# Two norms of a decoder step: the mean over channels as one product of a sum of seven chunks and one product of the eighth chunk

## The chip, the core and the metric

The kernel runs on one core of one Trainium2 chip. The metric is the device time of one execution in microseconds, the median of three runs. The profiled execution is a further one, recorded instruction by instruction; its times are microseconds from its own start.

## The reference

One step of a two-layer decoder trunk over 512 new prompt tokens and 8 x 4 sample tokens, width 1024. The part that matters here is the first layer's convolution module and the norm behind it:

```python
def rms_norm(x, g):
    return x * lax.rsqrt(jnp.mean(x * x, axis=-1, keepdims=True) + EPS) * g

def layer_norm(x, g, b):
    mu = jnp.mean(x, axis=-1, keepdims=True)
    var = jnp.mean(jnp.square(x - mu), axis=-1, keepdims=True)
    return (x - mu) * lax.rsqrt(var + EPS) * g + b

def conformer_conv(h, past, w_in, b_in, w_dw, b_dw, ln_g, ln_b, w_out, b_out):
    a, gate = jnp.split(h @ w_in + b_in, 2, axis=-1)
    ext = jnp.concatenate([past, a * jax.nn.sigmoid(gate)], axis=1)
    y = causal_dwconv(ext, w_dw, b_dw)                  # width 31, each channel by itself
    y = jax.nn.silu(layer_norm(y, ln_g, ln_b))
    return y @ w_out + b_out, ext[:, -(CONV_WIDTH - 1):]
...
x = x + conformer_conv(rms_norm(x, norm_mix[0]), ...)
x = x + conv_ffn(rms_norm(x, norm_ffn[0]), ...)
# layer 1: stick-breaking attention over paged keys and values, and again conv_ffn
```

## The kernel before

Activations lie transposed: 1024 channels are 8 chunks of 128 partitions, and the 544 tokens are the free dimension, cut into two streams, SA of 256 tokens (h = 0) and SB of 288 tokens (h = 1). A product in full precision is three passes of matmuls on the split operands whi, wlo (weights) and XH, XL (activations); lines L730 to L732 issue them, 8 chunks x 3 for one output chunk of one stream. Weights arrive by DMA as `raw`, ScalarE casts the high part (L374) and VectorE subtracts it for the low part (L377).

The first stage, some 200 us, is written down as a list of operations with dependencies and estimated costs (`plan.op(engine, cost, ...)`), and `Plan.run` puts them in order: at each step it takes the operation that can start earliest by the estimates, weighted by urgency and by the length of the chain behind it. Each engine then executes its own list strictly in that order. So an operation added or removed anywhere can move others, on all engines. What follows the stage (two ConvFFNs, the attention, the last norm) is ordered by plans of its own.

In the stage, for each chunk c and stream h:

- four products at a time (`conv_in`) give two chunks of `a` and two of the gate; L763, L765, L767 and L769 multiply, apply the sigmoid and write the result into `ext_p` (L773 for the sample tokens, `glu_s`).
- The depthwise convolution of chunks 0 and 1 is done on VectorE by 31 taps (L814, L818). Chunks 2 to 7 go through TensorE: `shifted` writes the chunk to DRAM (L832) and reads it back four times shifted into `rep` (L836), and `conv_tensor` multiplies 32 blocks by small diagonal weights `wdg` (L867, 32 matmuls of 32 columns, in two halves of 16); ScalarE copies the result out of PSUM (L872). Sample tokens are convolved on VectorE (L791, L796, with a bias on ScalarE, L798).
- The result `y` replaces `ext_p`. `add_sum` adds the chunks into `ysum` on VectorE (L884, seven adds per stream), and `layer_norm` takes the mean over channels by one product of `ysum` with a matrix of 1/1024 (L900), subtracts it (L908), squares on ScalarE (L910), adds pairs of squares (L915) and multiplies them with the same matrix (L918, four products). Then come the square root (L922), the reciprocal (L924), eight multiplies (L929), Silu (L931) and the split into XH and XL (L933, L934), which the output product `conv_out` reads (L730 to L732 again, evacuated by L1224 into xT).
- The norm in front of the ConvFFN squares xT (L1205 in `normed`), adds the squares up, on GpSimd and the last of a stream on VectorE (L1212), and for stream SA multiplies the sum with the matrix of 1/1024 (L1235). The second stream's norm is finished in the ConvFFN's plan.

PSUM tiles have tags: `acc` (four banks) for products, `tr` (two) for means and variances, `av` (two) for convolutions.

Of the kernel before, what the change touches and what calls it, by code (L numbers as in the profile page):

```python
# [19 lines left out]
NC = D // P  # L20
# [44 lines left out]
LIFT = 10  # L65
# [161 lines left out]
def tile_trunk(  # L227
# [9 lines left out]
    dve, act, pool, pe = nc.vector, nc.scalar, nc.gpsimd, nc.tensor  # L237

    def open_pool(name, bufs=1, space=None, side=None):
        kw = dict(name=name, bufs=bufs, reuse_waits="tile")  # L240
        if space is not None:
            kw["space"] = space
        if side is not None:
            kw["side"] = side
        cm = tc.tile_pool(**kw)
        return cm, cm.__enter__()
# [151 lines left out]
    mean_m = base.tile([P, P], F32, name="mean_m")  # L398
# [26 lines left out]
    def pcol(row, c):  # L425
        return prm[:, c, row:row + 1]
# [174 lines left out]
    yc = ext_p  # L601
# [8 lines left out]
    start_cm, start = open_pool("start")  # L610
# [84 lines left out]
    plan = Plan(E_CONV, 0.12)  # L695
    STREAMS = (SA, SB)
    late = {}

    def buf(pool_, tag, shape, bufs):
        name = pool_ if isinstance(pool_, str) else None  # L700
        b = plan.tile(tag, bufs, lambda: late.get(name, pool_).tile(shape, F32, tag=tag, name=uid(tag), bufs=bufs))
        if name:
            b.after |= {late["op"]}
        return b
# [3 lines left out]
    def psum(tag):  # L708
        def make():
            if tag == "acc":  # L710
                taken.append(tag)
            return bank(tag, uid(tag))

        return plan.tile(tag, banks[tag], make)

    def on(eng, n, dve_cost, pool_cost):
        return (dve, "dve", 0.08 + n * dve_cost) if eng == "dve" else (pool, "pool", 0.1 + n * pool_cost)
# [157 lines left out]

    def add_sum(c, h):
        c0, n = STREAMS[h]
        if c == 0:
            return
        keys = [("y", i, k) for i in ((0, 1) if c == 1 else (c,)) for k in ((1, 2) if h else (0,))]  # L880

        def add():
            o = late["ysum"][:, c0:c0 + n]
            dve.tensor_tensor(o, yc[:, c, c0:c0 + n], yc[:, 0, c0:c0 + n] if c == 1 else o, op=ALU.add)  # L884

        plan.op("dve", 0.08 + n * 1.05e-3, add, r=keys, w=[("sum", h)])

    def table(name):
        plan.op("act", 1.3, lambda: act_table(name), w=["table"])

    def layer_norm(h):

        c0, n = STREAMS[h]
        cols = slice(c0, c0 + n)
        urgent = URGENT
        mu, va = psum("tr"), psum("tr")
        rs = buf("ctmp", "dwa", [P, SEQ], 2)
        ycut = [("y", c, k) for c in range(NC) for k in ((1, 2) if h else (0,))]
        per = len(ycut) // NC
        plan.op("pe", n * 1.68e-3, lambda: pe.matmul(  # L900
            mu()[:, :n], mean_m, late["ysum"][:, cols], start=True, stop=True),
                r=[("sum", h)], w=[mu], urgent=urgent, lift=0.0 if h else LIFT)
        for c in range(NC):
            y = yc[:, c, cols]
            keys = ycut[c * per:(c + 1) * per]
            first = c % SQUARES == 0
            sq = buf("ctmp", "sqn", [P, SB[1]], 3)
            plan.op("dve", 0.1 + n * 1.12e-3, lambda y=y: dve.tensor_tensor(y, y, mu()[:, :n], op=ALU.subtract),  # L908
                    r=[mu], w=keys, urgent=urgent)
            plan.op("act", 0.1 + n * 0.9e-3, lambda y=y, sq=sq: act.activation(sq()[:, :n], y, AF.Square),  # L910
                    r=keys, w=[sq], urgent=urgent)
            if first:
                acc = sq
            else:
                plan.op("dve", 0.08 + n * 1.05e-3, lambda sq=sq, acc=acc: dve.tensor_tensor(  # L915
                    acc()[:, :n], sq()[:, :n], acc()[:, :n], op=ALU.add), r=[sq], w=[acc], urgent=urgent)
            if (c + 1) % SQUARES == 0:
                plan.op("pe", n * 1.68e-3, lambda c=c, acc=acc: pe.matmul(  # L918
                    va()[:, :n], mean_m, acc()[:, :n], start=(c < SQUARES), stop=(c == NC - 1)),
                    r=[acc], w=[va], urgent=urgent)  # L920
        table("sqrt_and_others")
        plan.op("act", 0.1 + n * 0.95e-3, lambda: act.activation(  # L922
            rs()[:, :n], va()[:, :n], AF.Sqrt, bias=eps_t[:, 0:1], scale=1.0), r=[va, "table"], w=[rs], urgent=urgent)
        plan.op("dve", 0.1 + n * 6.2e-3, lambda: dve.reciprocal(rs()[:, :n], rs()[:, :n]), w=[rs], urgent=urgent)  # L924
        table("silu_and_others")
        for c in range(NC):
            y = yc[:, c, cols]
            keys = ycut[c * per:(c + 1) * per]
            plan.op("dve", 0.08 + n * 1.05e-3, lambda y=y: dve.tensor_tensor(y, y, rs()[:, :n], op=ALU.mult),  # L929
                    r=[rs], w=keys, urgent=urgent)  # L930
            plan.op("act", 0.25 + n * 0.9e-3, lambda c=c, y=y: act.activation(  # L931
                y, y, AF.Silu, bias=pcol(R_LNB, c), scale=pcol(R_LNG, c)), r=["table"], w=keys)
            plan.op("act", 0.1 + n * 0.82e-3, lambda c=c, y=y: act.copy(XH[:, c, cols], y), r=keys, w=[("XH", c, h)])  # L933
            plan.op("dve", 0.08 + n * 1.05e-3, lambda c=c, y=y: dve.tensor_tensor(  # L934
                XL[:, c, cols], y, XH[:, c, cols], op=ALU.subtract), r=[("XH", c, h), *keys], w=[("XL", c, h)])
# [142 lines left out]
    for c in range(0, NC, 2):  # L1078
# [9 lines left out]
        for cc in range(2):  # L1088
            plan.op("act", 0.33, lambda c=c, cc=cc, pt=pt: act.copy(
                ext_s[:, c + cc, :, 0:PAST], pt()[:, cc * 240:(cc + 1) * 240].rearrange("p (b t) -> p b t", b=NB)),  # L1090
                r=[pt, "junk"], w=[("past", c + cc)])
# [40 lines left out]
    for h in range(2):  # L1132
        for c in range(NC):
            add_sum(c, h)

    layer_norm(0)

    def state(new):
# [22 lines left out]
    nrm = Norm(R_FFN, later=True)  # L1161
# [39 lines left out]
    def normed(c, h):  # L1201

        c0, n = STREAMS[h]
        sq = plan.tile("sq" if c else "sqa", 2, lambda: nrm.tile("sq" if c else "sqa", 2))
        plan.op("act", 0.1 + n * 0.9e-3, lambda: act.activation(sq()[:, :n], xT[:, c, c0:c0 + n], AF.Square),  # L1205
                r=[("x", c, h), "norm"], w=[sq])
        if c == 0:
            nrm.acc[h] = sq
            return
        a = nrm.acc[h]  # L1210
        e, name, cost = on("dve" if c == NC - 1 else "pool", n, 1.05e-3, 2.25e-3)
        plan.op(name, cost, lambda: e.tensor_tensor(a()[:, :n], sq()[:, :n], a()[:, :n], op=ALU.add), r=[sq], w=[a])  # L1212
# [3 lines left out]
    for h, (c0, n) in enumerate(STREAMS):  # L1216
        if h:
            layer_norm(1)
        for g in (0, 4):
            for i in range(4):  # L1220
                c = g + i
                pt = product(s0 + c, h)
                x = xT[:, c, c0:c0 + n]
                plan.op("dve", 0.1 + n * 1.12e-3, lambda c=c, n=n, x=x, pt=pt: dve.scalar_tensor_tensor(  # L1224
                    x, pt()[:, :n], pcol(R_BOUT, c), x, op0=ALU.add, op1=ALU.add), r=[pt, ("x0", c, h)], w=[("x", c, h)])
                normed(c, h)
        if not h:
            state(False)
            state(True)
            for f0 in (0, 8, 16):  # L1230
                ffn_rows(f0, min(8, NF - f0))
    table("sqrt_and_others")
    ms, rs = psum("tr"), plan.tile("rstd", 2, lambda: nrm.tile("rstd", 2))
    n = SA[1]
    plan.op("pe", 0.53, lambda: pe.matmul(ms()[:, :n], mean_m, nrm.acc[0]()[:, :n], start=True, stop=True),  # L1235
            r=[nrm.acc[0]], w=[ms])
    plan.op("act", 0.34, lambda: act.activation(rs()[:, :n], ms()[:, :n], AF.Sqrt, bias=eps_t[:, 0:1], scale=1.0),
            r=[ms, "table"], w=[rs])
    plan.op("dve", 1.7, lambda: dve.reciprocal(rs()[:, :n], rs()[:, :n]), w=[rs])
    for c in range(NC):  # L1240
# [3 lines left out]
                r=[rs, ("x", c, 0)], w=[u])  # L1244
# [4 lines left out]
            r=[u, ("XH", c, 0)], w=[("XL", c, 0)], lift=NLIFT)  # L1249
# [802 lines left out]
    plan = Plan()  # L2052
# [433 lines left out]
    for i, tag in enumerate(("acc", "z", "z", "one")):  # L2486
# [3 lines left out]
        for q in range(4):  # L2490
            last = plan.op("pe", 6 * SA[1] * COL, weighted(pt, o0 + i, 0, q), w=[pt], follows=last,
                           r=[("slot", o0 + i)] + [("X", k) for k in (2 * q, 2 * q + 1)])
# [13 lines left out]
    nrm = Norm(R_FFN + 1)  # L2506
# [12 lines left out]
    nrm = ffn(1, nrm, Final)  # L2519
# [35 lines left out]
```

## Time and profile before

| | us |
|---|---|
| median of three runs | 1274.54 (1273.38 to 1275.0) |
| profiled execution, its own time | 1274.43 |
| its span, first to last instruction | 1272.7 |
| TensorE busy in it | 1259.1 |
| VectorE busy in it | 1002.8 |
| ScalarE busy in it | 717.7 |

In the profile PE is TensorE's matmuls, PEld its weight loads, DVE VectorE, ACT ScalarE, POOL GpSimd and SP the DMA queue of the sync engine. A row of the timeline gives start, duration, engine, line, operation, output and inputs; in brackets stands how long the engine was idle before it and what ended that. A float32 matmul of the mean or of the convolution appears as two instructions. The matmuls of a stream overlap in the records, so the step from one start to the next tells what one costs. In this execution the granted TensorE clock was 0.998 of full speed.

### The profile page before, as it was taken

What the parts mean: (1) busy time and instruction counts of PE and PEld (TensorE: products, weight loads), DVE (VectorE), ACT (ScalarE), POOL (GpSimd) and SP (SyncE); (2) the same over time, 40 slices, a digit from 0 to 9 for tenths busy, and PEclk for the clock granted to TensorE, in tenths of its full rate; (3) what the DMA queues carried; (4) which work ended last, traced back from release to release, by engine and by line L of the source; (5) the groups of instructions that cost most, each with busy time, mean ns of one, the idle gap of its engine ahead of it and who ended that gap; (6) DMA issues with size and microseconds to landing.
All of it is one profiled execution on the core that took longest, in us unless ns stands there. A gap on an engine that the chain in (4) does not pass through costs nothing. (4 is left out here: it accounts for less than half of the span.)

```text
span 1272.7 us, 26479 instructions
## 1 busy us (share of the span) xinstructions
PE 1259.1 (99%) x10846; PEld 1209.1 (95%) x10846; DVE 1002.8 (79%) x1696; ACT 717.7 (56%) x1436; POOL 165.8 (13%) x291
## 2 busy tenths in 40 slices
PE   9999999999999999999999999999999999999998
PEld 8997789999999999999999888899999999999998
DVE  6999877888987886879865589766988987886863
ACT  6596574545655454445565488754645655454453
POOL 5000014111001000001042143200111001000000
PEclk9999999999999999999999999999999999999999
DMA  7464333023233232244354544342223233232221
GB/s 220 122 188 131 92 102 116 28 91 103 87 112 117 67 112 91 91 143 156 126 187 137 157 142 147 113 139 78 64 88 109 88 105 117 67 117 88 89 77 71
DMA packets 119180, 142.39 MB, mean 112 GB/s; under 512 B 5102, under 2 KB 110246, under 8 KB 118787
## 3 DMA queue, kind: packets, MB, share of 16 engines
q1 hardware_dynamic: 110350, 111.89, 28.3%
q0 software_dynamic: 8704, 28.80, 7.2%
q8 instruction: 85, 1.39, 0.5%
q14 instruction: 37, 0.30, 0.1%
q10 hardware_dynamic: 4, 0.01, 0.0%
HBM read 129.34 MB, written 12.18 MB: 111 GB/s over the span
## 5 line engine op out<-in xcount | busy, mean ns | idle before, releaser
L374 ACT CAST whi<-raw 128x1024 fp32r<-128x1024 f32 (+2 forms) x247 | 224.7, 913 | 118.0 <-PE av L1377 25.1
L377 DVE TENSOR_TENSOR wlo<-raw,whi 128x1024 fp32r<-128x1024 f32 (+2 forms) x247 | 258.5, 1049 | 28.6 <-ACT whi L374 27.2
L730 PE MATMUL acc<-XH,whi 128*128 128x288 f32 (+1 forms) x384 | 114.1, 297 | 0.0
L731 PE MATMUL acc<-XL,whi 128*128 128x288 f32 (+1 forms) x384 | 110.5, 288 | 0.1
L732 PE MATMUL acc<-XH,wlo 128*128 128x288 f32 (+1 forms) x384 | 110.3, 287 | 0.1
L1376 PE MATMUL av<-HH,whi 128*128 128x288 f32 (+1 forms) x280 | 83.2, 297 | 0.4 <-DVE xT L1691 0.4
L1602 PE MATMUL acc<-TH,wlo 128*128 128x272 f32 x288 | 83.0, 288 | 0.0
L1600 PE MATMUL acc<-TH,whi 128*128 128x272 f32 x288 | 82.8, 288 | 0.0
L1601 PE MATMUL acc<-TL,whi 128*128 128x272 f32 x288 | 82.7, 287 | 0.0
L1377 PE MATMUL av<-HL,whi 128*128 128x288 f32 (+1 forms) x280 | 82.6, 295 | 0.0
L2100 PE MATMUL acc<-XH,whi 128*128 128x256 f32 (+1 forms) x264 | 82.0, 311 | 0.6 <-ACT kT L2138 0.6
L1378 PE MATMUL av<-HH,wlo 128*128 128x288 f32 (+1 forms) x280 | 82.3, 294 | 0.0
L1636 ACT COPY G<-acc 128x272 f32<-128x272 f32 (+1 forms) x72 | 26.8, 372 | 94.7 <-PE acc L1602 94.7
L1376 PE MATMUL tr<-HH,whi 128*128 128x256 f32 (+1 forms) x280 | 79.1, 283 | 0.0
L1377 PE MATMUL tr<-HL,whi 128*128 128x256 f32 (+1 forms) x280 | 78.9, 282 | 0.0
L1378 PE MATMUL tr<-HH,wlo 128*128 128x256 f32 (+1 forms) x280 | 78.5, 280 | 0.0
L2102 PE MATMUL acc<-XH,wlo 128*128 128x256 f32 (+1 forms) x264 | 75.8, 287 | 0.0
L2101 PE MATMUL acc<-XL,whi 128*128 128x256 f32 (+1 forms) x264 | 75.8, 287 | 0.0
L730 PEld LDWEIGHTS acc<-XH,whi 128*128 128x128 f32 x384 | 72.2, 188 | 2.8 <-issue 1.6
L731 PEld LDWEIGHTS acc<-XL,whi 128*128 128x128 f32 x384 | 72.2, 188 | 1.0 <-DVE XL L982 0.3
L732 PEld LDWEIGHTS acc<-XH,wlo 128*128 128x128 f32 x384 | 72.1, 188 | 0.3 <-DVE wlo L377 0.3
L1539 DVE SCALAR_TENSOR_TENSOR cv<-G,fprm,cv 128x560 f32<-128x560 f32 x88 | 69.4, 796 | 0.5
(465 smaller groups left out, 4374.1 us busy)
## 6 DMA issues: line engine op xcount, KB each, us to landing
raw<-in_ffn_w_gate_dram SPq DMA_DIRECT2D x22, 1024.0 KB
raw<-in_ffn_w_up_dram SPq DMA_DIRECT2D x22, 1024.0 KB, 5.4
raw<-in_ffn_w_down_dram SPq DMA_DIRECT2D x24, 768.0 KB, 4.5
raw<-in_attn_w_qkv_dram SPq DMA_DIRECT2D x12, 1024.0 KB, 5.0
raw<-in_conv_w_in_dram POOLq DMA_DIRECT2D x6, 1024.0 KB, 6.5
rep<-glu SPq DMA_DIRECT2D x36, 142.0 KB, 3.6
raw<-in_conv_w_out_dram POOLq DMA_DIRECT2D x4, 1024.0 KB, 6.5
raw<-in_ffn_w_down_dram SPq DMA_DIRECT2D x8, 512.0 KB
```

The lines of the kernel that those rows point to most:

```text
L374: act.copy(hi[:, k, :], src[:, k])
L377: dve.tensor_tensor(lo[:, k, :], src[:, k], hi[:, k, :], op=ALU.subtract)
L730: pe.matmul(o, hi[:, k, :], XH[:, k, c0:c0 + n], start=(k == 0), stop=False)
L731: pe.matmul(o, hi[:, k, :], XL[:, k, c0:c0 + n], start=False, stop=False)
L732: pe.matmul(o, lo[:, k, :], XH[:, k, c0:c0 + n], start=False, stop=(k == NC - 1))
L1376: pe.matmul(o, hi[:, j + k, :], xh, start=(start and k == 0), stop=False, **kw)
L1377: pe.matmul(o, hi[:, j + k, :], xl, start=False, stop=False, **kw)
L1378: pe.matmul(o, lo[:, j + k, :], xh, start=False, stop=(stop and k == len(xs) - 1), **kw)
L1600: pe.matmul(o, hi[:, j + k, :], xh, start=(start and k == 0), stop=False, **kw)
L1601: pe.matmul(o, hi[:, j + k, :], xl, start=False, stop=False, **kw)
L1602: pe.matmul(o, lo[:, j + k, :], xh, start=False, stop=(k == 3), **kw)
L2100: pe.matmul(o, hi[:, k, :], XH[:, k, c0:c0 + n], start=(k == 0), stop=False)
```

## The change

In both norms the last chunk is no longer added to the sum on VectorE. The mean is one product of the sum of the first seven chunks and a second product of the last chunk, accumulated into the same PSUM tile. For the layer norm this holds for both streams, for the norm in front of the ConvFFN for stream SA alone. Three VectorE adds go and three products come; the planner's cost for the last norm's product is set to 0.45 for each of two, where it was 0.53 for one. Behind the change the planner orders the stage anew.

```diff
     def add_sum(c, h):
         c0, n = STREAMS[h]
-        if c == 0:
+        if c in (0, NC - 1):
             return
...
         plan.op("pe", n * 1.68e-3, lambda: pe.matmul(
-            mu()[:, :n], mean_m, late["ysum"][:, cols], start=True, stop=True),
+            mu()[:, :n], mean_m, late["ysum"][:, cols], start=True, stop=False),
                 r=[("sum", h)], w=[mu], urgent=urgent, lift=0.0 if h else LIFT)
+        plan.op("pe", n * 1.68e-3, lambda: pe.matmul(
+            mu()[:, :n], mean_m, yc[:, NC - 1, cols], start=False, stop=True),
+                r=ycut[-per:], w=[mu], urgent=urgent, lift=0.0 if h else LIFT)
...
         if c == 0:
             nrm.acc[h] = sq
             return
+        if c == NC - 1 and not h:
+            nrm.last = sq
+            return
...
-    plan.op("pe", 0.53, lambda: pe.matmul(ms()[:, :n], mean_m, nrm.acc[0]()[:, :n], start=True, stop=True),
-            r=[nrm.acc[0]], w=[ms])
+    for i, part in enumerate((nrm.acc[0], nrm.last)):
+        plan.op("pe", 0.45, lambda i=i, part=part: pe.matmul(
+            ms()[:, :n], mean_m, part()[:, :n], start=not i, stop=bool(i)), r=[part], w=[ms])
```

In the changed kernel the lines behind the first product of the mean have other numbers: the second product is L903, the subtraction L911, the adds of squares L918, the products of the variance L921 and the last norm's products L1242.

With the dependencies alone, the product of the sum can start when the seventh chunk is added, and only the product of the eighth chunk waits for that chunk.

## The prediction

> **What bounds the kernel now.** I read the page first: busy shares, clock, chain of work.
>
> ```profile
> PE 1259.1 (99%) x10846; PEld 1209.1 (95%) x10846; DVE 1002.8 (79%) x1696; ACT 717.7 (56%) x1436; POOL 165.8 (13%) x291
> PEclk9999999999999999999999999999999999999999
> PE 30%; DVE 4%; issue 0%; ACT 0%; DMA 0%; DVEq 0%
> ```
>
> PE is busy for 1259.1 of 1272.7 us at full clock, so 13.6 us of idle are all that any reordering can win. What the change puts on PE is paid in full unless it fills idle. Next the windows over the stage that the first planner lays out (columns: stretch, length, then busy PE, PEld, DVE, ACT, POOL, clock, DMA share, GB/s).
>
> ```profile
> 120.00:135.00 15.00, 13.84 (x236) 8.64 (x228) 14.05 (x21) 3.63 (x12) 0.00 (x0) 1.00 0.53 120
> 135.00:150.00 15.00, 14.80 (x122) 13.86 (x126) 9.71 (x24) 6.57 (x15) 0.88 (x1) 1.00 0.15 41
> 150.00:166.00 16.00, 14.84 (x249) 9.61 (x242) 15.51 (x29) 15.79 (x31) 0.88 (x1) 1.00 0.62 185
> 166.00:180.00 14.00, 13.79 (x106) 13.06 (x107) 10.20 (x19) 7.37 (x15) 1.47 (x2) 1.00 0.50 154
> 180.00:200.00 20.00, 19.82 (x157) 19.33 (x156) 16.56 (x31) 14.60 (x31) 7.80 (x10) 1.00 0.08 21
> ```
>
> Length less PE busy: 1.16 + 0.20 + 1.16 + 0.21 + 0.18 = 2.9 us idle, in both norms that change. The timeline of PE says where (start, duration, operation; in brackets the idle before it).
>
> ```profile
> 135.20 0.70 PE L900 MATMUL tr<-ysum,mean_m 128*128 128x256 f32 x2 [1.35 <-DVE ysum L884]
> 156.66 3.66 PE L867 MATMUL av<-rep,wdg 128*32 128x256 f32 x64 [0.90 <-DMA rep<-glu]
> 160.49 3.66 PE L867 MATMUL av<-rep,wdg 128*32 128x256 f32 x64 [0.17 <-issue]
> 191.85 0.70 PE L1235 MATMUL tr<-sqa,mean_m 128*128 128x256 f32 x2 [0.18 <-DVE sqa L1212]
> ```
>
> The mean of the first stream waits 1.35 us for the last DVE add, two convolutions wait 1.07 us, the last norm waits 0.18 us, and some 0.3 us is scattered.
>
> **The products added.** Three mean products (layer norm of both streams, last norm of the first) against three DVE adds. A product inside the stream:
>
> ```profile
> 138.11 0.59 PE L918 MATMUL tr<-sqn,mean_m 128*128 128x256 f32 x2
> 138.35 0.48 PE L730 MATMUL acc<-XH,whi 128*128 128x288 f32 x1
> 138.67 0.29 PE L731 MATMUL acc<-XL,whi 128*128 128x288 f32 x1
> 138.81 0.30 PE L732 MATMUL acc<-XH,wlo 128*128 128x288 f32 x1
> ```
>
> From 138.11 to 138.67 less one ordinary pitch of 0.13 is 0.43 us; 288 columns I scale to 0.48. Sum 0.43 + 0.48 + 0.43 = 1.34 us, on PE's path. Ends: 1.0 (three times the 138.35 - 138.11 = 0.24 and the 0.1 by which 138.67 is late) and 2.1 (three times the 0.70 busy of L900).
>
> **The adds removed.** They are 0.4 us each on DVE:
>
> ```profile
> 134.72 0.43 DVE L884 TENSOR_TENSOR ysum<-ext_p,ysum 128x256 f32<-128x256 f32 x1 [0.68 <-ACT ext_p L872]
> 191.38 0.42 DVE L1212 TENSOR_TENSOR sqa<-sq,sqa 128x256 f32<-128x256 f32 x1
> ```
>
> They count only through the waits behind them, the 1.35 and 0.18 us above. The second product of the last norm now stands where L1235 stood, and its input comes one add earlier: I count that wait as gone.
>
> **The order that moves.** The planner reorders the whole stage. DVE at the first mean, before and then after (L763, L767, L769 gate a product into ext_p; L791 and L796 convolve the samples; L884 adds a chunk to ysum):
>
> ```order
> L796 TENSOR_REDUCE ext_p<-prod_1931 128x32
> L791 TENSOR_TENSOR prod_1957<-ext_s,prm 128x992
> L884 TENSOR_TENSOR ysum<-ext_p,ysum 128x256
> L796 TENSOR_REDUCE ext_p<-prod_1957 128x32
> L839 MEMSET rep_1998 32x4
> L884 TENSOR_TENSOR ysum<-ext_p,ysum 128x256
> L908 TENSOR_TENSOR ext_p<-ext_p,tr_2016 128x256 x4
> ```
>
> ```order
> L796 TENSOR_REDUCE ext_p<-prod_1870 128x32
> L791 TENSOR_TENSOR prod_1910<-ext_s,prm 128x992
> L884 TENSOR_TENSOR ysum<-ext_p,ysum 128x288
> L791 TENSOR_TENSOR prod_1914<-ext_s,prm 128x992
> L884 TENSOR_TENSOR ysum<-ext_p,ysum 128x256
> L884 TENSOR_TENSOR ysum<-ext_p,ysum 128x288
> L767 TENSOR_TENSOR va_1946<-acc_1561,rstd 128x256
> L769 SCALAR_TENSOR_TENSOR ext_p<-va_1946,prm,sg_1890 128x256
> ```
>
> The add of the seventh chunk, now the last before the mean, stands among the same DVE work; the gate of the eighth chunk moved behind it. So when does that add run, and when does PE arrive?
>
> ```profile
> 98.50 0.28 PE L730 MATMUL acc<-XH,whi 128*128 128x256 f32 x1
> 101.18 0.28 PE L732 MATMUL acc<-XH,wlo 128*128 128x256 f32 x1
> 101.39 3.66 PE L867 MATMUL av<-rep,wdg 128*32 128x256 f32 x64
> 105.20 0.28 PE L731 MATMUL acc<-XL,whi 128*128 128x256 f32 x1
> 105.32 0.28 PE L732 MATMUL acc<-XH,wlo 128*128 128x256 f32 x1
> 114.59 17.47 PE L867 MATMUL av<-rep,wdg 128*32 128x256 f32 x320
> 98.69 0.42 DVE L767 TENSOR_TENSOR va<-acc,rstd 128x256 f32<-128x256 f32 x1 [0.30 <-PE acc L732]
> 99.04 0.74 DVE L814 SCALAR_TENSOR_TENSOR dwa<-ext_p,prm,dwa 128x512 f32<-128x512 f32 x1
> 132.40 0.42 DVE L884 TENSOR_TENSOR ysum<-ext_p,ysum 128x256 f32<-128x256 f32 x1
> ```
>
> PE is the same up to 98.50. From there to the mean the new order has one convolution, four, one, and 66 short products. Five convolutions in a row take 17.47, one 3.49; a lone one takes 105.20 - 101.18 less two pitches of 0.12 = 3.78, so 0.29 us goes with entering and leaving a group. PE arrives at 98.5 + 3.78 + 14.25 + 3.78 + 66 x 0.117 = 128.0. DVE: from 98.69 to the seventh chunk's add at 132.40 the new order drops one L767 (0.35), one L769 (0.40), one L796 (1.10), one long tap L814 (0.7), one add (0.38) and two memsets, has one L773 more (0.16), and runs its taps in longer chains (estimate 0.5 slower): about 2.4 less. The add starts at 130.0, and PE follows 135.20 - 134.72 = 0.48 later, at 130.5. So PE waits 2.5 us where it waited 1.35. Ends: 0.8, if each side is off by a little under 1 us, and 3.5. Both waiting engines have nothing else: behind the mean on PE stand the end of the eighth chunk's product and 84 products of the second stream, all late with it.
>
> PE behind the mean, before and after (L867 is the convolution; L921, which was L918, a product of the variance):
>
> ```order
> L732 MATMUL acc_2018<-XH,wlo_1281 128x288
> L867 MATMUL av_2159<-rep_1883,wdg_1100 32x256 x32
> L867 MATMUL av_2218<-rep_1952,wdg_1239 32x256 x32
> L867 MATMUL av_2273<-rep_1998,wdg_1518 32x256 x32
> L867 MATMUL av_2327<-rep_2237,wdg_1708 32x256 x32
> L730 MATMUL acc_2374<-XH,whi_1483 128x256
> ```
>
> ```order
> L867 MATMUL av_2138<-rep_2039,wdg_1099 32x256 x16
> L921 MATMUL tr_2171<-sqn_2135,mean_m 128x256
> L867 MATMUL av_2138<-rep_2039,wdg_1099 32x256 x16
> L921 MATMUL tr_2171<-sqn_2159,mean_m 128x256
> L867 MATMUL av_2205<-rep_2110,wdg_1232 32x256 x16
> L921 MATMUL tr_2171<-sqn_2196,mean_m 128x256
> L867 MATMUL av_2205<-rep_2110,wdg_1232 32x256 x16
> L921 MATMUL tr_2171<-sqn_2231,mean_m 128x256
> L867 MATMUL av_2266<-rep_2161,wdg_1521 32x256 x32
> L867 MATMUL av_2314<-rep_2223,wdg_1691 32x256 x16
> L900 MATMUL tr_2342<-ysum,mean_m 128x288
> L867 MATMUL av_2314<-rep_2223,wdg_1691 32x256 x16
> ```
>
> The four convolutions that ran in one group now stand between the products of the first variance, cut by five full-array products; one more group elsewhere costs 0.29. For the five cuts the trace has no row: 0 to 0.29 each, I take 0.15. Sum 0.29 + 0.75 = 1.0 us, ends 0.3 and 1.7. The Trainium skill, TensorEngine Tiling (Array Packing), Key Properties, says that changing the tiling mode drains TensorE; by that rule each cut costs the full 0.29 and the whole sum is 0.7 higher, and the 0.29 at the edge of a group agrees with it.
>
> New waits there. The third variance product will wait for DVE, which has this between the second and the third add of squares:
>
> ```profile
> 149.32 0.48 DVE L769 SCALAR_TENSOR_TENSOR ext_p<-va,prm,sg 128x256 f32<-128x256 f32 x1
> 149.72 0.25 DVE L773 SCALAR_TENSOR_TENSOR glu_s<-va,prm,sg 128x32 f32<-128x32 f32 x1
> 149.88 1.18 DVE L796 TENSOR_REDUCE ext_p<-prod 128x32 f32<-128x992 f32 x1
> 150.98 1.22 DVE L377 TENSOR_TENSOR wlo<-raw,whi 128x1024 fp32r<-128x1024 f32 x1
> 152.11 1.18 DVE L791 TENSOR_TENSOR prod<-ext_s,prm 128x992 f32<-128x992 f32 x1
> 153.21 1.74 DVE L924 RECIPROCAL dwa<-dwa 128x256 f32<-128x256 f32 x1
> 154.99 2.77 DVE L929 TENSOR_TENSOR ext_p<-ext_p,dwa 128x256 f32<-128x256 f32 x8
> 155.80 1.09 ACT L931 ACTIVATE ext_p<-ext_p,prm 128x256 f32<-128x256 f32 x2
> ```
>
> L769 to L377 take 152.11 - 149.32 = 2.8, with the add 3.2; PE has half a convolution and a product, 1.75 + 0.43 = 2.2, and some 0.4 in hand from the two before: 0.65 wait. The second stream's mean (its last add stands behind reciprocal and eight multiplies, 1.78 + 2.77, and PE has 5.7 us of work since the last variance product): about 0.35. The last chunk of that mean waits for an evacuation that ACT does behind two L931 (1.09): about 0.5. Together 1.5, ends 0.5 and 3. The convolutions' 1.07 us goes, since their transfers now start well ahead, except in the rival below. Waits: 2.5 + 1.5 = 4.0 for 2.9 before, +1.1.
>
> **Sum.** 1.34 + 1.0 + 1.1 = +3.4 us. The profiled execution took 1274.43 (its span 1272.7, 1.7 around it), the median of the runs is 1274.54: I predict 1277.8. With all low ends: 1.0 + 0.3 + (1.3 - 2.9) = -0.3; all high: 2.1 + 1.7 + (6.5 - 2.9) = +7.4.
>
> **Rivals.** First, not slower: DVE and PE meet at the first mean. If PE comes 1 us later or the add 1 us sooner, and cuts cost nothing, the waits stay at 2.9 and the sum is 1.34 + 0.3 = +1.6 or less: 1276.0, inside 0.2% (2.5 us, about what a measurement of this kernel can tell). For it: my 128.0 counts no wait between 98.5 and there. It decides from a wait of 1.6 us at that mean. Second, faster: the split ends all of the 2.9 us: 1.34 + 0.3 - 2.9 = -1.3, 1273.2. Beyond 0.2% it would need more idle than the stage has. Third, the last convolution's transfer is late again:
>
> ```profile
> 149.83 0.34 SPq L832 DMA_DIRECT2D glu<-ext_p  x1
> 155.87 1.73 SPq L836 DMA_DIRECT2D rep<-glu  x4
> ```
>
> Six us passed here between the two steps beside a weight load. Now the gate of the last chunk runs some 5 us after the variance begins; with such a transfer that convolution waits 2.3 us more: 1280.1. Fourth, the idle at the mean grows past 3 us and the clock falls: with 27 products at half rate after it, 27 x 0.13 = 3.5 us more and the longer gap 1.0, 1282.3. Against it: 1.35 us of idle left the clock row at 9. The Trainium skill, TensorE: Matmul & The Clock Gate, HAM oscillation, names 3.4 us of idle; no run here shows it.
>
> **Chances.** Forecast 0.38, first rival 0.42, second (beyond 0.2%: 0.05) 0.07, third 0.10, fourth 0.03. Slower by over 0.2%: 0.38 + 0.10 + 0.03 and a little of the first, 0.53; faster 0.05; within 0.42. The range from 1273.9 to 1281.0 leaves out most of the second rival, the fourth, and the third's far end; the forecast's own is 1276.5 to 1279.5.
>
> **What would show it.** After: idle of about 2.5 us before the first L900 near 130; idle before the third variance product; L867 still near 3.5 us each; three mean products more of 0.43; DVE's last adds gone. The prediction is wrong if idle over 120 to 200 us is 2.9 or less, or if the first variance starts at 136 as now, instead of near 148.

## The result and the profile after

| | before | changed |
|---|---|---|
| median | 1273.81 us (1272.84 to 1275.28, 22 runs) | 1276.83 us (1275.23 to 1278.46, 22 runs) |
| ratio, 95% interval | | 1.0019 (1.0013 to 1.0025) |
| profiled execution, span | 1274.43, 1272.7 us | 1277.50, 1275.7 us |

The medians lie 3.0 us apart; by the interval of the ratio the change costs 1.7 to 3.2 us. The forecast was +3.4, and the first rival's figure +1.6: the result lies between the two. The busy times on the page of the changed kernel:

```profile
PE 1263.0 (99%) x10852; PEld 1210.1 (95%) x10852; DVE 1003.5 (79%) x1693; ACT 717.3 (56%) x1436; POOL 166.6 (13%) x291
```

PE is busy 3.9 us longer in a span that is 3.0 longer, so idle fell. The page's clock digits are all 9, as before, but each covers a slice of 32 us, in which a dip of a few us is lost. The same five windows as before:

```profile
120.00:135.00 15.00, 12.71 (x123) 10.71 (x123) 11.26 (x16) 2.20 (x6) 0.00 (x0) 0.89 0.09 29
135.00:150.00 15.00, 15.00 (x151) 12.98 (x153) 9.88 (x16) 5.49 (x11) 1.76 (x2) 1.00 0.86 232
150.00:166.00 16.00, 15.90 (x234) 8.18 (x226) 15.26 (x33) 11.79 (x28) 0.00 (x0) 1.00 0.47 119
166.00:180.00 14.00, 14.00 (x127) 12.57 (x127) 11.36 (x25) 11.91 (x25) 0.84 (x1) 1.00 0.24 76
180.00:200.00 20.00, 19.97 (x159) 19.51 (x159) 15.07 (x26) 14.02 (x30) 6.21 (x9) 1.00 0.20 61
```

Length less PE busy is 2.29 + 0 + 0.10 + 0 + 0.03 = 2.42 us of idle, against 2.90 before. All of it but 0.13 stands in the first window, which also has a clock of 0.89. In windows of 1 us:

```profile
130.00:131.00 1.00, 0.96 (x6) 0.91 (x7) 0.35 (x1) 0.00 (x0) 0.00 (x0) 0.95 0.00 0
131.00:132.00 1.00, 1.00 (x6) 1.00 (x6) 0.18 (x1) 0.00 (x0) 0.00 (x0) 0.50 0.00 0
134.00:135.00 1.00, 1.00 (x8) 1.00 (x8) 0.00 (x0) 0.00 (x0) 0.00 (x0) 0.84 0.84 295
```

A window at 0.95 is at half speed for a tenth of it, one at 0.84 for 0.32: TensorE ran at half its clock from 130.90 to 134.32, 3.42 us, and 6 matmuls lie in a window of 1 us where 10 are usual. That takes away up to 1.7 us of work. The timeline of PE (to be read beside the prediction's rows):

```profile
130.04 0.70 PE L900 MATMUL tr<-ysum,mean_m 128*128 128x256 f32 x2 [2.29 <-DVE ysum L884]
152.32 1.93 PE L867 MATMUL av<-rep,wdg 128*32 128x256 f32 x32
154.18 0.70 PE L921 MATMUL tr<-sqn,mean_m 128*128 128x256 f32 x2
154.81 1.94 PE L867 MATMUL av<-rep,wdg 128*32 128x256 f32 x32
156.67 0.70 PE L921 MATMUL tr<-sqn,mean_m 128*128 128x256 f32 x2
159.80 5.50 PE L867 MATMUL av<-rep,wdg 128*32 128x256 f32 x96
```

The wait at the first mean is there, 2.29 us. No bracket stands at the third variance product (156.67) or at the last convolutions. Half a convolution and a variance product take 154.81 - 152.32 = 2.49 us. The prediction named two signs that would prove it wrong, and the first came: idle over 120 to 200 us is 2.42, where it said that 2.9 or less would do so. The second did not: the first variance product starts at 151.69 us, near the forecast 148.

Two profiled executions can't be laid on each other from zero, since the wait for the input's first transfer differs. A landmark of both is the ACT table load, near 21 us and again behind the stage. First before, then the changed kernel:

```profile
21.54 1.28 ACT L458 ACT_TABLE_LOAD   x1
226.06 1.28 ACT L458 ACT_TABLE_LOAD   x1
```

```profile
20.86 1.28 ACT L458 ACT_TABLE_LOAD   x1
229.14 1.28 ACT L458 ACT_TABLE_LOAD   x1
```

From load to load it is 204.52 and 208.28 us: the stage is 3.76 us longer, 0.7 more than the spans say. From the second load to the end of the span it is 1046.64 and 1046.56, so nothing is lost or won behind the stage. These lengths come from one execution of each kernel, and the landmark is ACT's. Read on TensorE itself, between two products that both kernels have (L730 at 60.03 and L732 at 212.12 us before, 59.66 and 215.20 after), the stage is 3.45 us longer; so differences between landmarks are good to some 0.3 us.

### The profile page after: what moved, and what is told of

Its sections match the earlier page's. It is cut to its first block, busy times and chain, and to the rows that moved or that the text cites. A ratio compares the mean times of both kernels' runs of the same rounds, so it can differ in the third digit from the quotient of the medians.

```text
span 1275.7 us, 26478 instructions
## 1 busy us (share of the span) xinstructions
PE 1263.0 (99%) x10852; PEld 1210.1 (95%) x10852; DVE 1003.5 (79%) x1693; ACT 717.3 (56%) x1436; POOL 166.6 (13%) x291
## 5 line engine op out<-in xcount | busy, mean ns | idle before, releaser
L377 DVE TENSOR_TENSOR wlo<-raw,whi 128x1024 fp32r<-128x1024 f32 (+2 forms) x247 | 258.8, 1051 | 29.8 <-ACT whi L374 28.1
L730 PE MATMUL acc<-XH,whi 128*128 128x288 f32 (+1 forms) x384 | 114.4, 298 | 0.0
L732 PE MATMUL acc<-XH,wlo 128*128 128x288 f32 (+1 forms) x384 | 111.0, 289 | 0.1
L730 PEld LDWEIGHTS acc<-XH,whi 128*128 128x128 f32 x384 | 72.9, 190 | 3.1 <-issue 2.1
L732 PEld LDWEIGHTS acc<-XH,wlo 128*128 128x128 f32 x384 | 72.8, 190 | 0.3 <-DVE wlo L377 0.3
```

What stands on the lines that cost most here:

```text
L377: dve.tensor_tensor(lo[:, k, :], src[:, k], hi[:, k, :], op=ALU.subtract)
L730: pe.matmul(o, hi[:, k, :], XH[:, k, c0:c0 + n], start=(k == 0), stop=False)
L732: pe.matmul(o, lo[:, k, :], XH[:, k, c0:c0 + n], start=False, stop=(k == NC - 1))
```

## The experiments

The theories after the result: the wait at the mean is as forecast, the waits behind it are not, and a half clock came in their place. What each part costs, when the clock falls, and whether the wait must be there is what the runs were for. Steps added to DVE (a maximum of a value with itself) and products on PE that are written over change nothing in the output. Each comparison is with the kernel before, run beside it.

**The products alone.** The kernel before; each of the three means issues its product twice.

```diff
-        plan.op("pe", n * 1.68e-3, lambda: pe.matmul(
-            mu()[:, :n], mean_m, late["ysum"][:, cols], start=True, stop=True),
+        plan.op("pe", n * 1.68e-3, lambda: [pe.matmul(
+            mu()[:, :n], mean_m, late["ysum"][:, cols], start=True, stop=True) for _ in range(2)],
```

> The kernel before with its order untouched; each of the three means (layer norm of both streams, last norm of the first stream) issues its one product twice, the second overwriting the first. Theory (the products cost what they cost inside a stream, the rest of the change's time is order and waits): +1.3 to +1.5 us, idle before the mean as before, 1.35 us, clock 1.00 throughout. Rival (the split's products run where TensorE idles anyway and cost nothing): 0 us. Rival (a product costs its recorded 0.70 us): +2.1 us.

Measured 1274.89 us against 1274.43, ratio 1.0005 (0.9996 to 1.0014), which holds both nothing and 1.34 us. In the timeline:

```profile
134.74 1.13 PE L900 MATMUL tr<-ysum,mean_m 128*128 128x256 f32 x4 [1.36 <-DVE ysum L884]
```

One product more is 1.13 - 0.70 = 0.43 us. From landmark to landmark the stage is 0.92 us longer. The price of one product was right; the total can't be told apart.

**The half clock taken away.** The changed kernel, with 18 products of zeros ahead of the first mean, so that PE is busy in its wait.

```diff
+        plan.op("pe", n * 1.68e-3, lambda: [*(pe.matmul(
+            mu()[:, :2 * P], zero[:, :P], zero, start=True, stop=True) for _ in range(0 if h else 18)), pe.matmul(
-        plan.op("pe", n * 1.68e-3, lambda: pe.matmul(
```

> The changed kernel, order untouched; ahead of the first stream's product of the sum stand 18 small bf16 products of zeros (256 columns) into the same PSUM tile, which wait for nothing and are overwritten. They fill about 2.1 of the 2.3 us in which TensorE waits for VectorE. Theory (the long idle halves the TensorE clock for some 3.3 us behind it, which costs about 1.6 us): granted clock stays 1.00 between 127 and 136 us and the time falls by about 1.5 us against the changed kernel, to +1.5 us over before. Rival (the halved clock has another cause, or costs nothing since other engines set the time there): +3.0 us as the changed kernel.

Measured 1275.73 us against 1274.43, 1.0015 (1.0006 to 1.0024). As a time that is +0.8 to +3.1 us, which holds the +1.5 of the theory and the +3.0 of its rival, so only the trace decides. The windows behind the mean have their clock, and a wait appears at the last convolution:

```profile
130.00:131.00 1.00, 0.82 (x5) 0.77 (x6) 0.49 (x2) 0.00 (x0) 0.00 (x0) 1.00 0.00 0
162.00:163.00 1.00, 0.05 (x4) 0.00 (x0) 1.00 (x4) 1.00 (x4) 0.00 (x0) 1.00 0.05 14
```

```profile
163.54 1.93 PE L867 MATMUL av<-rep,wdg 128*32 128x256 f32 x32 [1.49 <-ACT XH L937]
```

In this execution, the slowest of eleven, the 1.5 us came back as a wait. The last window has a DMA share of 0.05, about one of 16 engines at work, and from 163.0 on there is none; the cast that the bracket names has no part in that convolution, so I take the wait for the end of its transfer, by inference. That would be the prediction's third rival. No run of the eleven has a mean clock of 0.997 or less, which 7 of the 22 of the changed kernel have. The median of these 7 is 1277.44 us, of the other 15 it is 1276.26.

The mean clock of a run is a rough sign only. Every trace also has the half clock in the last 2.0 to 4.8 us of its span, behind the last products, so that a mean of 0.999 is a run without another fall, 0.997 one with a fall somewhere, and 0.998 can be either (the trace with one more DVE step, below, has a fall at the mean and 0.998).

**The split in the layer norm alone.** The changed kernel with the last norm put back; the order in the stage is that of the change.

```diff
-        if c == NC - 1 and not h:
-            nrm.last = sq
-            return
         a = nrm.acc[h]
...
-    for i, part in enumerate((nrm.acc[0], nrm.last)):
-        plan.op("pe", 0.45, lambda i=i, part=part: pe.matmul(
-            ms()[:, :n], mean_m, part()[:, :n], start=not i, stop=bool(i)), r=[part], w=[ms])
+    plan.op("pe", 0.53, lambda: pe.matmul(ms()[:, :n], mean_m, nrm.acc[0]()[:, :n], start=True, stop=True),
+            r=[nrm.acc[0]], w=[ms])
```

> Only the two means of the layer norm are split, the last norm stays as before; the order of the stage is that of the change. Theory (the cost lies in the layer norm: cuts of convolutions, products, and the half clock): between 0.1 and 0.5 us under the change itself, that is +2.2 to +2.9 us over before, and the half clock after the first mean again in a part of the executions. Rival (the last norm carries a good part of the cost): +1.5 us or less.

Measured 1276.22 us against 1274.21, 1.0014 (1.0005 to 1.0023): +2.0, between the theory and the rival, and the interval (+0.6 to +2.9) reaches into both. But the profiled execution was the fastest of its eleven:

```profile
20.75 1.28 ACT L458 ACT_TABLE_LOAD   x1
226.47 1.28 ACT L458 ACT_TABLE_LOAD   x1
```

```profile
129.64 0.70 PE L900 MATMUL tr<-ysum,mean_m 128*128 128x256 f32 x2 [2.28 <-DVE ysum L884]
```

```profile
131.00:132.00 1.00, 1.00 (x10) 1.00 (x9) 0.89 (x2) 0.00 (x0) 0.00 (x0) 1.00 0.00 0
```

The same order and the same wait, 2.28 us, and the clock stays whole. From landmark to landmark it is 205.72, +1.20 over before. So the length of the wait alone does not decide the fall. Three of the eleven runs have a mean clock of 0.997. The last convolutions wait for nothing here (no bracket from 157.85 on), although TensorE has its clock: the late transfer of the experiment before does not follow from the whole clock.

**The split in the last norm alone.** The changed kernel with the layer norm put back.

```diff
-        if c in (0, NC - 1):
+        if c == 0:
...
-            mu()[:, :n], mean_m, late["ysum"][:, cols], start=True, stop=False),
+            mu()[:, :n], mean_m, late["ysum"][:, cols], start=True, stop=True),
                 r=[("sum", h)], w=[mu], urgent=urgent, lift=0.0 if h else LIFT)
-        plan.op("pe", n * 1.68e-3, lambda: pe.matmul(
-            mu()[:, :n], mean_m, yc[:, NC - 1, cols], start=False, stop=True),
-                r=ycut[-per:], w=[mu], urgent=urgent, lift=0.0 if h else LIFT)
```

> Only the last norm's mean is split, the layer norm stays as before. Theory: one product of 0.43 us more, 0.18 us of wait less: +0.2 us, within 0.6 us of before. Rival (the last norm carries a good part): +1.0 us or more.

Measured 1275.43 us, 1.0008 (0.9999 to 1.0017): +1.2, and 1.09 from landmark to landmark. That is the rival's side (+1.0 or more), though the interval (-0.1 to +2.2) holds the theory too. The wait I counted as gone stays in this order, now for the square:

```profile
191.49 0.70 PE L1239 MATMUL tr<-sq,mean_m 128*128 128x256 f32 x2 [0.21 <-ACT sq L1205]
198.70 0.40 PE L731 MATMUL acc<-XL,whi 128*128 128x288 f32 x1 [0.44 <-DVE XL L934]
```

A second wait, 0.44 us for a split that DVE does, stands some 7 us behind it. With 0.65 us of idle in place of 0.18, and 0.43 for the product, 0.9 of the 1.09 is found. In the changed kernel itself these waits are gone: no bracket stands at its two products of the last norm.

The two parts, 1.20 and 1.09, are 2.3 of the change's 3.76. The rest, 1.5, is what the half clock takes by the rows of the changed kernel: 15 steps of its products from 130.94 to 134.40 took 3.46 us, where the usual steps of 0.117 and 0.132 make 1.93. Neither part's profiled execution has the half clock. But the sum is an argument, not a measurement: the second part's waits don't stand in the changed kernel, and by the landmarks on TensorE the rest is 1.0.

**Both products late.** The changed kernel; the first product waits for the last chunk too, and the planner keeps the order of before, with five groups of convolutions.

```diff
-                r=[("sum", h)], w=[mu], urgent=urgent, lift=0.0 if h else LIFT)
+                r=[("sum", h), *ycut[-per:]], w=[mu], urgent=urgent, lift=0.0 if h else LIFT)
```

> The changed kernel, but the product of the sum is also told to wait for the last chunk, so that the planner puts both products of a mean side by side; its order of the stage then comes out close to that of the kernel before (first mean near 135 us, the four convolutions in one group). The two adds of the layer norm are gone as in the change. Theory (the order costs, by the longer wait, the halved clock and the cut group; the products cost 1.3 us): +1.0 to +1.6 us over before, no half clock. Rival (the split as such costs, whatever the order): +3 us.

Measured 1278.12 us against 1274.43, 1.0032 (1.0019 to 1.0044): +3.7, a miss; the rival's +3 lies in the interval.

```profile
132.72 0.70 PE L900 MATMUL tr<-ysum,mean_m 128*128 128x256 f32 x2 [0.46 <-DVE ysum L884]
134.67 0.67 PE L903 MATMUL tr<-ext_p,mean_m 128*128 128x256 f32 x2 [1.25 <-ACT ext_p L872]
135.00:136.00 1.00, 1.00 (x8) 0.97 (x7) 0.62 (x2) 0.17 (x1) 0.00 (x0) 0.82 0.00 0
139.00:140.00 1.00, 1.00 (x8) 0.95 (x7) 0.00 (x0) 0.28 (x1) 0.00 (x0) 0.97 0.00 0
```

The last chunk's evacuation ends the wait, not the add: two waits of 0.46 and 1.25 us in 2.4 us were enough for the half clock, from 135.64 to 139.06, again 3.42 us. The last two convolutions wait as well, 1.06 and 1.60 us (at 158.59 and 163.85). These four waits are 4.4 us, where the kernel before had 2.4 at the same places. So this run does not show that the new order is what costs. That the split need not cost 3 us in every order is shown by the last version below.

**The wait made longer.** The kernel before with one, three and six more DVE steps of 0.46 us behind the first mean's last add.

```diff
+            for _ in range(3 if c == NC - 1 and not h else 0):
+                dve.tensor_tensor(o, o, o, op=ALU.max)
```

> Before, with one more DVE step of 0.46 us behind the last add of the first mean (three such steps left 2.74 us of idle there). The idle should be 1.35 + 0.46 = 1.8 us. Theory (the clock falls only from an idle between 1.8 and 2.3 us on): full clock behind the mean and +0.5 us. Rival (1.8 us is enough already): granted clock 0.5 for about 3 us behind the mean and +1.5 to +2.1 us.

> The kernel before, order untouched; behind the last add of the first stream's sum stand three more VectorE steps on the same tile, each the maximum of the sum with itself, so that the mean comes about 1.1 us later and TensorE idles some 2.4 us instead of 1.35. Theory (an idle of 2.3 us and more halves the clock, one of 1.35 us does not): granted clock 0.50 for about 3.3 us behind the mean and +2.5 us in all. Rival (the clock does not follow from the idle): +1.1 us, clock 1.00.

> Before, with six more DVE steps of 0.46 us behind the last add of the first mean: 1.35 + 6 x 0.46 = 4.1 us of idle. Theory (the clock is set for stretches of 3.4 us by how busy TensorE was in the stretch before, and where the stretches begin is chance; an idle of 4.1 us covers over 2 us of one stretch wherever they begin): the clock falls in every run, all at a mean clock of 0.997 or less, +2.8 + 1.6 = +4.4 us and little spread. Rival (the fall is chance at any length of idle): a part of the runs only, +2.8 to +4.4 us.

| steps | idle at the mean | half clock in the trace | runs at 0.997 or less | median, ratio |
|---|---|---|---|---|
| 0 | 1.35 us | none | 2 of 89 | |
| 1 | 1.82 | 3.42 us | 4 of 11 | 1275.56, 1.0010 (1.0001 to 1.0019) |
| 3 | 2.74 | 3.42 us | 7 of 11 | 1276.75, 1.0020 (1.0011 to 1.0029) |
| 6 | 4.13 | 6.82 us | 3 of 5 | 1278.64, 1.0035 (1.0022 to 1.0049) |

The 89 runs are those of the kernel before that ran beside the experiments. The trace with three steps has one more half clock, from 7.81 to 11.23 us, which adds to its count. The rows of one step, and of six:

```profile
135.78 1.17 PE L902 MATMUL tr<-ysum,mean_m 128*128 128x256 f32 x2 [1.82 <-DVE ysum L886]
135.00:136.00 1.00, 0.22 (x1) 0.22 (x2) 0.69 (x2) 0.00 (x0) 0.00 (x0) 0.93 0.00 0
139.00:140.00 1.00, 1.00 (x8) 1.00 (x8) 1.00 (x5) 0.18 (x1) 0.00 (x0) 0.86 0.00 0
```

```profile
138.44 1.22 PE L902 MATMUL tr<-ysum,mean_m 128*128 128x256 f32 x2 [4.13 <-DVE ysum L886]
136.00:137.00 1.00, 0.00 (x0) 0.00 (x0) 0.93 (x3) 0.00 (x0) 0.00 (x0) 0.81 0.00 0
143.00:144.00 1.00, 1.00 (x8) 0.97 (x6) 0.11 (x1) 0.00 (x0) 0.00 (x0) 0.78 0.00 0
```

With one step the half clock lasts from 135.86 to 139.28, with six from 136.62 to 143.44: once and twice 3.41 us. The theory of one step (that 1.8 us is too little) fell, its rival held in the trace; the median, +1.35, lies between them, and its interval (+0.1 to +2.4) tells neither from the other. With three steps +2.3 was measured for +2.5, and the trace has the half clock. The theory of six steps was right on the time (+4.38 for +4.4, interval +2.8 to +6.2, which holds the rival's figures as well) and not clearly on the count: two of five runs show 0.998, where one fall of 3.4 us moves the mean clock by 0.0013 and the record has three digits. The Trainium skill, TensorE: Matmul & The Clock Gate, Part 1, describes an activity window of 3.4 us that runs freely; the lengths of 3.42 and twice 3.41 agree with it. Its figure of a whole idle window does not: 1.82 us sufficed here.

The traces also show what decides between a fall and none at the same wait. In each of the five traces with a fall at the mean, the fall at the end of the kernel comes a whole number of 3.413 us later, 333 or 334 of them: (1270.95 - 130.90) / 3.4133 = 334.0 in the changed kernel, (1272.50 - 135.86) / 3.4133 = 333.0 with one step. So the windows lie on one fixed grid through the whole execution, and the end of the kernel tells where it lies. The rows of the end, first of the changed kernel, then of the split in the layer norm alone:

```profile
1270.00:1271.00 1.00, 0.00 (x0) 0.00 (x0) 0.96 (x3) 0.69 (x1) 0.75 (x1) 0.98 0.00 0
1268.00:1269.00 1.00, 0.00 (x0) 0.00 (x0) 0.44 (x1) 0.04 (x1) 0.34 (x1) 0.76 0.32 125
```

The clock falls at some 1270.95 and 1268.52. In the changed kernel, 334 windows back is 130.9, where the fall at the mean came, and its whole wait of 2.29 us lies in the window ahead, from 127.5. In the other kernel a window ends at 128.47, in the middle of the wait from 127.36 to 129.64: 1.11 us lie in one window and 1.17 in the next, and neither was followed by a fall. Where the grid lies differs from one execution to the next, so the fall looks like chance.

**A cut by itself.** The kernel before, with a product of zeros ahead of every convolution, into the tile that the convolution then writes over.

```diff
             def f(m0=m0):
+                if m0 == 0:
+                    pe.matmul(pt()[:, :2 * P], zero[:, :P], zero, start=True, stop=True)
```

> Before, with one full-array product of zeros (0.12 us each, 18 of them took 2.14 us) ahead of each of the twelve convolutions, so that seven places inside the groups of five and four are cut. Theory (a cut costs the full 0.29 to 0.31 us): the group of five convolutions, 17.47 us before, takes 17.47 + 4 x 0.42 = 19.1 us, and the group of four 3 x 0.42 = 1.3 us more. Rival of the prediction (0.15 us each): 18.5 us; no cost of a cut at all: 17.9 us. The total depends on what the waits absorb: +1.5 to +4 us.

Measured 1274.89 us, 1.0004 (0.9995 to 1.0013). The first and the last of the group of five, and the mean behind it:

```profile
115.52 3.66 PE L869 MATMUL av<-rep,wdg 128*32 128x256 f32 x64
119.12 0.28 PE L866 MATMUL av<-zero 128*128 128x256 bf16 x1
...
130.75 3.66 PE L869 MATMUL av<-rep,wdg 128*32 128x256 f32 x64
136.03 0.59 PE L902 MATMUL tr<-ysum,mean_m 128*128 128x256 f32 x2
```

The group takes 130.75 + 3.66 - 115.52 = 18.89 us, between the two expectations: (18.89 - 17.47) / 4 = 0.355 for product and cut, less 0.12 is 0.24 for a cut. Some 3 us more on PE (12 x 0.12 + 7 x 0.24) moved the medians by only 0.7 us (interval -0.6 to +1.7), under the +1.5 to +4 expected. Part of the reason is that the mean lost its wait of 1.35 us: no bracket stands at 136.03. PE has over a us to spare ahead of that mean.

**DVE's adds elsewhere.** The kernel before, with the adds of chunks 1 to 5 of the first stream on GpSimd.

```diff
+            e = pool if c < 6 and not h else dve
-            dve.tensor_tensor(o, yc[:, c, c0:c0 + n], yc[:, 0, c0:c0 + n] if c == 1 else o, op=ALU.add)
+            e.tensor_tensor(o, yc[:, c, c0:c0 + n], yc[:, 0, c0:c0 + n] if c == 1 else o, op=ALU.add)
```

> Before, with the adds of chunks 1 to 5 of the first stream's sum (five of seven, some 0.4 us each on DVE) on GpSimd, which is idle there; the order on TensorE is that of before. Theory (TensorE waits at the first mean for DVE's work, so what leaves DVE ahead of it is gained): idle at the mean 0.3 us or less instead of 1.35, and -0.8 to -1.2 us. Rival (the gain is given back at the convolutions' transfers, or GpSimd slows DVE): -0.3 to +0.5 us with the idle moved elsewhere.

Measured 1274.58 us against 1274.26, 1.0000 (0.9991 to 1.0009): the rival held, but by neither of its reasons alone.

```profile
129.24 0.83 POOL L885 TENSOR_TENSOR ysum<-ext_p,ysum 128x256 f32<-128x256 f32 x1 [5.48 <-ACT ext_p L872]
129.39 0.99 DVE L885 TENSOR_TENSOR ysum<-ext_p 128x288 f32<-128x288 f32 x1
...
132.50 0.45 DVE L885 TENSOR_TENSOR ysum<-ext_p,ysum 128x288 f32<-128x288 f32 x1
...
133.10 1.19 DVE L796 TENSOR_REDUCE ext_p<-prod 128x32 f32<-128x992 f32 x1
134.37 0.32 ACT L798 ACTIVATE ext_p<-ext_p,prm 128x32 f32<-128x32 f32 x1 [2.12 <-issue]
134.60 0.46 ACT L872 ACTIVATE ext_p<-av,prm 128x256 f32<-128x256 f32 x1
135.14 0.43 DVE L885 TENSOR_TENSOR ysum<-ext_p,ysum 128x256 f32<-128x256 f32 x1
135.62 0.70 PE L901 MATMUL tr<-ysum,mean_m 128*128 128x256 f32 x2 [1.03 <-DVE ysum L885]
```

Beside the add on GpSimd a DVE add took 0.99 us instead of 0.45, which gives back the 0.4 us that one add saves; a split of weights on DVE (L377) beside another of these adds took 1.77 instead of 1.21. And the last rows are a chain: a reduce of sample tokens on DVE, its bias on ACT, the evacuation of the last convolution behind that on ACT, the add, the mean. Fewer adds early on don't shorten it.

**The planner's cost of a convolution.** It stands at 2.05 us for half a convolution, which takes 1.73. With 1.78, in the kernel before and in the changed one:

```diff
-            last = plan.op("pe", 2.05, f, follows=last, ...
+            last = plan.op("pe", 1.78, f, follows=last, ...
```

> Before, with the planner told 1.78 us instead of 2.05 for half a convolution (it takes 1.73 in a group). Six convolutions then stand in one group ahead of the first mean, four groups in all instead of five. Theory (entering and leaving a group costs about 0.3 us): -0.3 us, if the waits stay. Rival (the wait at the first mean moves with the order): +0.5 to +1.5 us.

> The changed kernel with the planner told 1.78 us instead of 2.05 for half a convolution: nine pieces of convolution work instead of eleven. Theory (a piece costs 0.3 us): 0.6 us under the change, +1.8 to +2.6 us over before, and if the wait at the first mean is under 1.7 us no half clock and +1.2 to +2.0. Rival (pieces cost nothing): +2.8 to +3.2 us as the change itself.

Before with 1.78: 1274.44 us, 1.0002 (0.9993 to 1.0011): +0.2, between the theory and the rival. The wait at the first mean is gone, but the last norm waits where it hardly had, and the products behind it wait too (0.84 and 1.04 us):

```profile
189.01 0.70 PE L1235 MATMUL tr<-sqa,mean_m 128*128 128x256 f32 x2 [1.18 <-DVE sqa L1212]
```

The change with 1.78: 1273.78 us (1272.14 to 1274.79), 0.9991 (0.9982 to 1.0000). It is the only version that came out under the kernel before; the interval just reaches 1. Its landmarks and its PE:

```profile
21.98 1.28 ACT L458 ACT_TABLE_LOAD   x1
224.98 1.28 ACT L458 ACT_TABLE_LOAD   x1
```

```profile
128.09 0.59 PE L900 MATMUL tr<-ysum,mean_m 128*128 128x256 f32 x2
120.00:135.00 15.00, 15.00 (x188) 12.13 (x181) 14.26 (x20) 3.24 (x7) 0.00 (x0) 1.00 0.15 47
150.00:166.00 16.00, 15.83 (x230) 9.33 (x221) 14.20 (x29) 11.68 (x29) 0.00 (x0) 1.00 0.23 66
```

The mean waits for nothing, the clock stays whole, and the stage takes 203.00 us, 1.52 less than before. The split is the same as in the change; only the order differs, in which the last adds come in time. Against before with the same planner's cost it is 0.7 us less by the medians, and the stage is 2.7 us shorter in the traces (203.00 against 205.67). Neither expectation went below +1.2 us: I had counted on fewer pieces and a whole clock, not on the end of nearly all waits.

## Why the prediction was right or wrong

- **The first mean: right.** TensorE came at 127.75 (128.0 forecast), the mean at 130.04 (130.5), and the wait is 2.29 us (2.5). The order and durations of the trace before gave this within half a us.
- **The products: right in price.** 0.43 us each in the double product; the three were put at 1.34 and no run contradicts that, though none shows the total. In the changed kernel the last norm waits for nothing, as forecast.
- **The cuts: too low, by price.** I took 0.15 of 0.29. A cut by itself measured 0.24. In the changed kernel half a convolution and a variance product take 2.49 us against 1.73 + 0.43, so 0.33. Yet the layer norm's part without the half clock is 1.20 us in all, with 0.4 less idle, so products and cuts together are about 1.6 where I had 0.91 + 1.0. The dearer cuts were made up for somewhere; it may be that the second stream's products run faster where no variance product interrupts them, but no run shows that by itself. The full 0.29 of a group's edge was nearer the price of a cut than my half of it. The Trainium skill's rule that a change of tiling drains TensorE (TensorEngine Tiling (Array Packing), Key Properties) has it paid at every cut; it names no price.
- **The new waits: wrong.** The third variance product, the second stream's mean and its last chunk were to wait 1.5 us together; the trace has 0.13 us of idle behind the first mean. The step that failed is "some 0.4 in hand": at the second variance product (154.18) TensorE was already 1.3 us later than the add that feeds it (done at 152.92), and the steps of 2.49 instead of 2.18 us gave DVE the rest. The convolutions' 1.07 us went as forecast. Waits came to -0.5 instead of +1.1 us, and by the prediction's own sign (idle of 2.9 us or less) its mechanism is wrong here.
- **The fourth rival: the mechanism came, from a shorter idle.** It was given 0.03, from 3 us of idle on, and 3.5 us of cost. It came from 1.82 us on, takes about 1.5, and comes in a part of the runs. I had read one row (1.35 us left the clock whole) as the rule for all shorter than 3. The reason given there, the clock row at 9, could not have shown such a fall; the windows at 1.00 did show that there was none.
- **The sum.** +3.4 was forecast and +3.0 measured, and that it came so near is in part luck: the waits were 1.6 us too high, and in the profiled execution the half clock, which the sum did not have, put about 1.5 us in their place. In the median of the runs it stands with a share only, since by their mean clock 7 of the 22 have a fall for certain and 10 have none. Products and cuts at 2.0, waits at -0.5 and the half clock make 3.0 of the 3.45 to 3.76 us between the landmarks; the rest is not traced.
- **The first rival, not slower**, needed a wait under 1.6 us at the mean. It was not met here; with another order it is, and the last version shows that the whole loss turned on the order. Which of its waits or pieces made the difference was not tested one by one. The second rival's reason, the end of all waits, is what the trace of that version shows, and its figure (1.3 us under before) lies between the 0.5 of the medians and the 1.5 from landmark to landmark. The third rival, the late transfer, stayed out of the changed kernel's trace. A wait like it shows in one trace with the whole clock (1.49 us) and not in the other.

## What to carry to other kernels

Ask of a removed step whether it lay on the chain that ends the wait, and where the planner will put the rest: the same split cost 3.0 us in one order and came out 0.5 under in another (with an interval that reaches zero), and one cost in the planner's table decided which. A wait of 2 us on TensorE is to be priced at more than its length, since it can halve the clock behind it, in those executions in which most of it falls into one window of the clock. An experiment that adds work and costs little (3 us for 0.7) tells how much an engine has to spare, and where.

## What the hardware showed

- TensorE's clock halved for 3.42 us, or twice that, after waits of 1.82, 2.29, 2.74 and 4.13 us, but not in every execution: with 2.28 and 2.29 us of wait in the same order it fell in one and not in the other, whose wait was cut by the clock's grid of 3.413 us into 1.11 and 1.17. Two waits of 0.46 and 1.25 us close together also did it; a single wait of 1.35 us left it whole in the traces (two of 89 runs of the kernel before have a mean clock of 0.997 or less, for a reason that no trace shows).
- In the five traces with a fall at the mean, the 3.42 us ahead of it hold 1.7 us or more of idle, about half (worked out from the rows: in the changed kernel 127.48 to 130.90, with 2.29 idle). The wait of 1.49 us at the last convolution, which lies in one window, left the clock whole. That about half a window is the rule is inferred from these; the exact bound stays open. It is not the idle time alone: at the kernel's start (three steps, 7.81 us) and at its end the clock fell behind windows with 1.4 and 1.0 us of idle, in which small products stand (down to 128x1 at the end).
- A change between convolution blocks of 32 columns and a full-array product costs 0.24 us a place when the product is a short bf16 one.
- An add on GpSimd took DVE's add beside it from 0.45 to 0.99 us.
